# A scan that reads its PSUM tiles with two engines: the masked read first, the plain copy second

## The chip, the cores and the metric

The kernel runs on one core of one Trainium2 chip. The metric is device time in microseconds; the median of three runs is compared. The profile comes from one execution of its own.

## The reference

One layer of a bidirectional diffusion backbone, batch 1, with 128 context tokens and 2048 latent tokens, width 1024, float32. The input is normalised and modulated, and one projection makes all inputs of two groups of channels:

```
h = rmsnorm(x, norm_g) * (1 + scale) + shift
r, k, v, g_a, b_gate, c_gate, u_conv, g_b = split(h @ w_in)
ya = wkv(h, shifted r, k, v, s0) * silu(g_a)      # 8 heads of 64, two directions
yb = b_gate * conv3(c_gate * u_conv) * silu(g_b)  # 512 channels
y  = rmsnorm(x + gate * (concat(ya, yb) @ w_out), final_g)
```

The part that matters here is `wkv`. For each head and each direction it runs a recurrence over the tokens with a state S of 64 x 64, and reads the state out at every token:

```
S = S * w_t - (S kk_t) (kk_t a_t)^T + v_t k_t^T
y_t = S r_t
```

Context tokens start from zero, latent tokens from a given state. The outputs are y for both token sets and the final states of the context.

## The kernel before

Phase 1 (to about 940 us) makes the projections and, per token, the factors of the recurrence, and spills them. Phase 3 (from about 1463 us) is the output projection. Between them lies the scan, `phase2`, which works on chunks of 64 tokens, so that the recurrence inside a chunk becomes matrix products.

The scan has 17 stages. A stage holds, for each of the two directions (`st.g`, two groups `g`), 8 units; a unit is a pair of heads and a chunk. Products of a stage are taken in two halves `n` of 4 units. For each half there are two PSUM tiles per product, one per direction, and they are read out like this:

- F (`partW`, L1017): one masked product on VectorE.
- G (`partW`): for each half `h` of the partitions, ScalarE copies columns 0 to 63 into `fg` (the helper `copy`, L825) and VectorE multiplies columns 64 to 127 with a mask into another slot of `fg` (L1025). A direction's G tile thus has four readers, two on each engine.
- U and W (`partU`): solve inside the chunk. `zr` is a transpose on VectorE (L1031), and `zb` is written by ScalarE (L1048, L823).
- X (`partB`): two negated copies per tile into `fg` on ScalarE (L823).
- E (`partB`): per half two sub-steps, each with one tile per direction. ScalarE copies one set of columns into `E` (L825), VectorE masks the other set (L1086). E has two readers.
- S (`partS`): the recurrence itself. Step `i` multiplies `E` with the state `sv`, and VectorE scales the result into the next unit's `sv` (L1123). The next step's product waits for this.
- `finish` normalises and gates a stage's output y: a square on ScalarE (L1171), a sum on VectorE (L1174), a root on ScalarE (L1175), a reciprocal and a product on VectorE (L1177, L1178), a transpose through TensorE and two more VectorE operations (L1191, L1193).

TensorE's order in the scan is written out by hand: each round r of a stage runs the string

```
ROUND = "f b L L S u b S b S S U S T U S L S B S L B B".split()
```

in which L is a step of F or G of the next stage, b is X or E of this stage's second half, B is X or E of the next stage's first half, u and U are steps of `partU`, S a step of the scan, f and T steps of `finish`. The last rounds use a similar string. So one round has, in TensorE's queue: X, F, G, S, E, S, E, S, S, U, S, (transpose), W, S, F, S, X, S, G, E, E. In what follows psG, psE and so on are the PSUM tiles of these products, and round r is the one whose psU belongs to stage r + 1.

VectorE's and ScalarE's queues are not written by hand. Instructions are recorded in program order and a scheduler places them by its own estimate of when they are ready. When two engines read the same PSUM tile, the one that comes second in the program is made to wait for the one that comes first, also if both only read. In rounds up to the 13th the scan's tiles rotate through five buffers, so the fifth tile after a G tile waits until both engines have read it; then it is three.

From round 12 on ScalarE and VectorE also split the output weights into two parts (`woh` L1330, `wol` L1331) in the same queues, and TensorE begins the output projection (psa).

Of the kernel before, what the change touches and what calls it, by code (L numbers as in the profile page):

```python
# [10 lines left out]
ALU = mybir.AluOpType  # L11
# [25 lines left out]
def place(d, h):  # L37

    x = 1 - h if d == 0 else h
    return slice(x * 64, x * 64 + 64)  # L40
# [708 lines left out]
def phase2(K):  # L749
    nc, tc, A, S = K.nc, K.tc, K.A, K.S  # L750
    V, G, P, T = nc.vector, nc.gpsimd, nc.scalar, nc.tensor
    D = nc.sync.dma_start
    B = Ctx()
# [4 lines left out]
    H = (slice(0, 64), slice(64, 128))  # L758
# [55 lines left out]
    def ps_tile(shape, name):  # L814

        O.n += 1
        if O.pm is not None and (O.n % 5 < 2 or O.p2 is None):
            return O.pm.tile(shape, F32, tag="m", name=name)
        return O.p2.tile(shape, F32, tag="s", name=name)

    def copy(dst, src, negate=False):
        if negate:
            P.activation(dst, src, AF.Copy, scale=-1.0)  # L823
        else:
            P.copy(dst, src)  # L825
# [6 lines left out]
    def mm(*a, **k):  # L832

        r = T.matmul(*a, start=True, stop=True, **k)  # L834
        K.first = r.ins
        if O.line:
            behind(r, O.last)
            O.last = r.ins
# [7 lines left out]
    def tl(shape, tag, b, pool=None, dt=F32):  # L846
        return (pool or O.l0).tile(shape, dt, tag=tag, name=f"{tag}_{K.u()}", bufs=b)
# [8 lines left out]
    def half(g, n):  # L856

        h = n if g.d == 0 else 1 - n
        return slice(h * 4, h * 4 + 4)
# [107 lines left out]
    def load_half(g, us, D):  # L967

        p, c0 = g.units[us.start]
        src = S[f"ops{g.d}"][1:3]  # L970
        for h in range(2):
            dst = B.fg[g.d][H[h], :, g.op, h, us].rearrange("c k u t -> c k (u t)")
            if g.blk is not None:
                D(dst, src[:, p * 128 + h * 64:p * 128 + h * 64 + 64, c0 * 64:(c0 + 4) * 64].rearrange("k c t -> c k t"))
            else:
                for k in range(2):
                    D(dst[:, k].rearrange("c (g t) -> c g t", t=128), src[k, :, 0:128].rearrange("(g h c) t -> h c g t", h=2, c=64)[h][:, p:p + 2])

    def states(s, st):

        D = nc.sync.dma_start if s else P.dma_start
        for g in st.g:
            g.sv = tl([128, 8, 2, 64], "sv", 4)
            load_v(g.sv[64:128], g.units, D)
            first_states(g, D)

    def partW(s, st):

        D = nc.sync.dma_start if s else P.dma_start
        for g in st.g:  # L990
            g.E, g.F = [], []
            g.op = 1 + s % 2
            g.io = slice(0, g.op + 1, g.op)
            g.gs, g.fs = B.fg[g.d][:, 0], B.fg[g.d][:, 1]
        for n in range(2):
            for g in st.g:
                load_half(g, half(g, n), D)
            if n == 0:
                if s:
                    states(s, st)  # L1000
                st.zc = tl([128, 16, 32], "zc", 1, O.r0)
                for h in range(2):
                    D(st.zc[h:128:2], S["zt"][s][h].rearrange("u s b q i -> (s b q) u i"))

            def product(k, x, nm):
                ps = [ps_tile([128, 4, 128], f"ps{nm}{s}_{gi}_{n}") for gi in range(2)]
                for i in range(4):
                    for gi, g in enumerate(st.g):
                        u = half(g, n).start + i
                        for h in range(2):  # L1010
                            mm(ps[gi][place(g.d, h), i, :].rearrange("p (b t) -> p b t", b=2), g.ops[H[h], k, u, :], B.fg[g.d][H[h], x, g.io, h, u])
                return ps

            ps = product(0, 1, "F")
            for gi, g in enumerate(st.g):
                g.F.append(tl([128, 4, 128], "F", 4, O.r0))
                V.tensor_tensor(g.F[n][:], ps[gi][:], B.mF[:, g.d].unsqueeze(1).broadcast_to((128, 4, 128)), ALU.mult)  # L1017
            yield
            ps = product(1, 0, "G")
            for gi, g in enumerate(st.g):  # L1020
                us = half(g, n)
                for h in range(2):
                    r = place(g.d, h)
                    copy(g.gs[H[1 - h], 0, h, us], ps[gi][r, :, 0:64])
                    V.tensor_tensor(g.gs[H[1 - h], g.op, h, us], ps[gi][r, :, 64:128], B.mG[r, g.d].unsqueeze(1).broadcast_to((64, 4, 64)), ALU.mult)  # L1025
            yield

    def partU(s, st):
# [28 lines left out]
    def partB(s, st):  # L1057
        for n in range(2):
            px = [ps_tile([128, 4, 128], f"psX{s}_{gi}_{n}") for gi in range(2)]
            for i in range(4):  # L1060
                for gi, g in enumerate(st.g):
                    u = half(g, n).start + i
                    for h in range(2):
                        r = place(g.d, h)
                        mm(px[gi][H[1 - h], i, :], B.zb[r, gi, u, :], g.F[n][r, i, :])
            for gi, g in enumerate(st.g):
                for h in range(2):
                    copy(g.fs[H[1 - h], g.io, h, half(g, n)], px[gi][H[1 - h]].rearrange("p u (b t) -> p b u t", b=2), True)
            yield
            for h2 in range(2):  # L1070
                for gi, g in enumerate(st.g):
                    if h2 == 0:
                        g.E.append(tl([128, 4, 2, 128], "E", 4))
                    us = half(g, n)
                    k = (h2 if g.d == 0 else 1 - h2) * 2
                    lt, rt = (g.fs, g.gs) if g.d == 0 else (g.gs, g.fs)
                    pe = ps_tile([128, 2, 2, 128], f"psE{s}_{gi}_{n}{h2}")
                    for i in range(2):
                        u = us.start + k + i
                        for hd in range(2):  # L1080
                            for x in range(2):
                                mm(pe[H[x], i, hd, :].rearrange("p (b t) -> p b t", b=2), lt[:, x * g.op, hd, u], rt[:, g.io, hd, u])
                    to = lambda c: g.E[n][:, k:k + 2, :, c].rearrange("p a b c -> p (a b) c")
                    of = lambda c: pe[:].rearrange("p a b c -> p (a b) c")[:, :, c]
                    copy(to(H[0]), of(H[0]))
                    V.tensor_tensor(to(H[1]), of(H[1]), B.mE[:, g.d].unsqueeze(1).broadcast_to((128, 4, 64)), ALU.mult)  # L1086
                yield

    def partS(s, st, nxt):
# [114 lines left out]
    def early():  # L1204
        setup_first()
        center_states()
        partI(2)
        B.back = O.solved
        yield
        sts[0] = partL(0, K.dense)  # L1210
        yield
        partI(3, K.dense)
        yield
        W, uu, bb = partW(0, sts[0]), partU(0, sts[0]), partB(0, sts[0])
        for gen in (W, W, uu, uu, uu):
            next(gen, None)
            yield
        partI(4, B.back)
        for gen in (bb, W, W):
            next(gen, None)  # L1220
            yield
        B.bb = bb

    def main():
# [13 lines left out]
        for s in range(NST):  # L1238
            st = sts.pop(s)
            more = s + 1 < NST  # L1240
            nil = iter(())
            W, uu = (partW(s + 1, sts[s + 1]), partU(s + 1, sts[s + 1])) if more else (nil, nil)
            own, bb = bb, partB(s + 1, sts[s + 1]) if more else nil
            todo = [pend.pop(0) for _ in range(len(pend) if s > NST - 4 else min(1, len(pend)))]
            if s == NST - 3:
# [235 lines left out]
```

## Time and profile before

| | |
|---|---|
| median of 3 runs | 1668.08 us (1666.92 to 1673.68) |
| profiled execution | 1662.38 us |
| its span, first to last instruction | 1660.6 us |
| granted TensorE clock, mean | 0.978 |
| busy: TensorE | 1548.4 us (93%) |
| busy: VectorE | 1077.8 us (65%) |
| busy: ScalarE | 767.6 us (46%) |

In the rows of the profile each line has the start and the length in us, the engine (PE is TensorE, DVE is VectorE, ACT is ScalarE, POOL is GpSimd; PEld is TensorE's loading of weights), the source line, the operation, what it writes and reads, and how many instructions are merged into the row. In square brackets stands how long the engine was idle before it and which engine's work ended the idle time. A row of the waits has who waited, for whom, then us in total, times, and the longest. A float32 matmul shows as two rows in the count. An operation can show as starting a little before the one ahead of it ends.

### The profile page before, as it was taken

The numbers are of one execution on the slowest core, as the hardware profiler recorded it, in microseconds if no ns is written. First come the engines' busy times: TensorE is split into PE (matmuls) and PEld (weight loads), VectorE is DVE, ScalarE is ACT, GpSimd is POOL, SyncE is SP. The second block draws the span as 40 slices with busy tenths as digits, with TensorE's granted clock in tenths as the row PEclk, the third lists the DMA queues.
The fourth block names the chain that finished last, engine by engine and source line by source line (L and its number), as shares of the span: only waits on it lengthen the run. The fifth ranks groups of instructions, "written<-read, shape, count | busy, mean of one in ns | idle before, by whom it ended". The sixth has DMA issues, their size and how long they took to land.

```text
span 1660.6 us, 42386 instructions
## 1 busy us (share of the span) xinstructions
PE 1548.4 (93%) x17160; PEld 1417.8 (85%) x17160; DVE 1077.8 (65%) x2122; ACT 767.6 (46%) x1623; POOL 615.9 (37%) x1134
## 2 busy tenths in 40 slices
PE   6899999999999999999999998988889988789998
PEld 2899998999999999999988997777777877668886
DVE  5876978784638776657788534676767765574343
ACT  4544565553425454435554024666576655432222
POOL 0011221110102111112775588888888840022221
PEclk9899999999999999999999999999999979889999
DMA  9677767665746465555858859566676643264342
GB/s 378 211 258 244 254 236 265 215 227 194 217 145 207 165 207 189 188 201 179 269 177 245 273 180 272 150 184 191 171 211 157 193 135 103 65 198 149 137 146 95
DMA packets 237859, 327.23 MB, mean 197 GB/s; under 512 B 91288, under 2 KB 191896, under 8 KB 223584
## 3 DMA queue, kind: packets, MB, share of 16 engines
q1 hardware_dynamic: 231552, 318.02, 59.6%
q0 software_dynamic: 1360, 4.46, 0.7%
q8 instruction: 135, 2.21, 0.5%
q10 hardware_dynamic: 4752, 2.04, 0.5%
q14 instruction: 60, 0.49, 0.1%
HBM read 207.92 MB, written 116.54 MB: 195 GB/s over the span
## 4 chain that ended last, share of the span: by engine, by line
PE 69%; DVE 14%; ACT 7%; issue 5%; DMA 3%; POOL 0%; SPq 0%; DVEq 0%; ACTq 0%; POOLq 0%
PE psu L1351 4%; PE psu L1350 4%; PE psu L1352 4%; PE psE L834 3%; PE psS L834 3%; ACT fg L823 3%; PE psA L377 2%; PE mmc L166 2%; PE mmc L167 2%; PE mmu L166 2%; PE mmc L168 2%; PE mmu L168 2%; PE mmu L167 2%; PE psX L834 2%; PE mmv L166 2%
## 5 line engine op out<-in xcount | busy, mean ns | idle before, releaser
L939 POOL TENSOR_TENSOR zt<-zt,ztmp 128x30 f32<-128x30 f32 (+7 forms) x450 | 179.5, 399 | 35.1
L834 PE MATMUL psE<-fg 128*64 128x128 f32 x2176 | 137.4, 280 | 20.9 <-DVE fg L1025 17.2
L834 PEld LDWEIGHTS psE<-fg 128*64 128x64 f32 x2176 | 123.1, 141 | 27.3 <-issue 22.0
L834 PE MATMUL psS<-sv,E 128*64 128x64 f32 x2176 | 107.1, 236 | 25.1 <-DVE sv L1123 21.7
L834 PEld LDWEIGHTS psS<-sv,E 128*64 128x64 f32 x2176 | 83.5, 143 | 48.2 <-DVE sv L1123 38.5
L329 POOL TENSOR_TENSOR shk<-rawl 128x384 f32<-128x384 f32 (+1 forms) x24 | 24.9, 1037 | 233.8 <-ACT rawl L325 214.6
L936 POOL TENSOR_TENSOR ztmp<-ab,zt 128x60 f32<-128x60 f32 (+7 forms) x195 | 99.7, 511 | 15.3
L823 ACT ACTIVATE fg<-psX 64x512 f32<-64x512 f32 x136 | 80.5, 592 | 40.5 <-PE psX L834 38.4
L1417 POOL TENSOR_TENSOR z<-z,x 128x512 f32<-128x512 f32 x32 | 41.7, 1303 | 139.4 <-DVE z L1413 114.6
L1123 DVE TENSOR_TENSOR sv<-psS,pc 64x128 f32<-64x128 f32 x254 | 67.8, 279 | 38.8 <-PE psS L834 36.2
L1025 DVE TENSOR_TENSOR fg<-psG,consts 64x256 f32<-64x256 f32 x136 | 56.8, 418 | 47.9 <-ACT fg L825 45.1
L329 POOL TENSOR_TENSOR shv<-rawl 128x384 f32<-128x384 f32 (+1 forms) x24 | 20.4, 852 | 161.9 <-ACT rawl L325 153.7
L825 ACT COPY E<-psE 128x256 f32<-128x256 f32 x136 | 47.7, 374 | 52.6 <-PE psE L834 43.5
L166 PE MATMUL mmg<-h,w 128*128 128x384 f32 (+1 forms) x192 | 63.6, 331 | 3.7 <-ACT q1v L327 3.7
L1017 DVE TENSOR_TENSOR F<-psF,consts 128x512 f32<-128x512 f32 x68 | 44.0, 680 | 34.6 <-PE psF L834 34.6
L166 PE MATMUL mmc<-h,w 128*128 128x384 f32 (+1 forms) x192 | 64.3, 335 | 2.3 <-ACT t L423 1.8
L1086 DVE TENSOR_TENSOR E<-psE,consts 128x256 f32<-128x256 f32 x136 | 54.5, 416 | 18.2 <-ACT E L825 16.7
L825 ACT COPY fg<-psG 64x256 f32<-64x256 f32 x136 | 49.9, 367 | 33.5 <-PE psG L834 16.9
L166 PE MATMUL mmb<-h,w 128*128 128x384 f32 (+1 forms) x192 | 63.1, 329 | 1.5 <-ACT ta L436 1.5
L443 POOL COPY pcs<-pp 128x6 f32<-128x6 f32 (+1 forms) x48 | 21.5, 450 | 115.3 <-ACT pp L432 115.0
L166 PE MATMUL mmgb<-h,w 128*128 128x384 f32 (+1 forms) x192 | 63.7, 332 | 0.3 <-ACT q1r L327 0.3
L166 PE MATMUL mmv<-h,w 128*128 128x384 f32 (+1 forms) x192 | 63.4, 330 | 0.2 <-ACT q1r L327 0.2
(316 smaller groups left out, 5144.9 us busy)
## 6 DMA issues: line engine op xcount, KB each, us to landing
w<-scr_wsp SPq DMA_DIRECT2D x68, 1024.0 KB, 5.5
scr_wsp<-w SPq DMA_DIRECT2D x34, 1024.0 KB, 4.9
scr_ops<-pair SPq DMA_DIRECT2D x80, 384.0 KB, 3.0
wr<-in_win SPq DMA_DIRECT2D x34, 512.0 KB, 5.9
o<-scr_ops SPq DMA_DIRECT2D x32, 512.0 KB, 7.0
fg<-scr_ops SPq DMA_DIRECT2D x120, 128.0 KB, 5.0
x<-in_x SPq DMA_DIRECT2D x17, 512.0 KB, 3.8
wadas<-in_wada SPq DMA_DIRECT2D x8, 1024.0 KB, 13.5
```

What stands on the lines that cost most here:

```text
L166: T.matmul(ps[:, :n], w[:, 0, k], hh[:, 0, k, :n], start=k == 0, stop=False)
L167: T.matmul(ps[:, :n], w[:, 0, k], hh[:, 1, k, :n], start=False, stop=False)
L168: K.dense = T.matmul(ps[:, :n], w[:, 1, k], hh[:, 0, k, :n], start=False, stop=k == 7).ins
L823: P.activation(dst, src, AF.Copy, scale=-1.0)
L825: P.copy(dst, src)
L834: r = T.matmul(*a, start=True, stop=True, **k)
L936: G.tensor_tensor(tv, ab[:, j:j + 2, j + 2:32].unsqueeze(1).broadcast_to((128, kn, 2, n)), zt[:, :kn, j:j + 2].unsqueeze(3).broadcast_to(( ...
L939: O.solved = G.tensor_tensor(zt[:, :kn, j + 2:32], zt[:, :kn, j + 2:32], tv[:, :, r], ALU.subtract).ins
L1123: r = V.tensor_tensor(dst, sp[gi][0:64, q], B.pc[0:64, d, 2 * p:2 * p + 2, c:c + 1].broadcast_to((64, 2, 64)), ALU.mult)
L1350: T.matmul(ps[:], mh[:, n], hi[:, cs], start=start and n == 0, stop=False)
L1351: T.matmul(ps[:], mh[:, n], lo[:, cs], start=False, stop=False)
L1352: T.matmul(ps[:], ml[:, n], hi[:, cs], start=False, stop=stop and n == 3)
```

## The change

In `partW` and in `partB` two statements change places. Each instruction and each access stays as it is.

```diff
                 for h in range(2):
                     r = place(g.d, h)
+                    V.tensor_tensor(g.gs[H[1 - h], g.op, h, us], ps[gi][r, :, 64:128], B.mG[r, g.d].unsqueeze(1).broadcast_to((64, 4, 64)), ALU.mult)
                     copy(g.gs[H[1 - h], 0, h, us], ps[gi][r, :, 0:64])
-                    V.tensor_tensor(g.gs[H[1 - h], g.op, h, us], ps[gi][r, :, 64:128], B.mG[r, g.d].unsqueeze(1).broadcast_to((64, 4, 64)), ALU.mult)
...
+                    V.tensor_tensor(to(H[1]), of(H[1]), B.mE[:, g.d].unsqueeze(1).broadcast_to((128, 4, 64)), ALU.mult)
                     copy(to(H[0]), of(H[0]))
-                    V.tensor_tensor(to(H[1]), of(H[1]), B.mE[:, g.d].unsqueeze(1).broadcast_to((128, 4, 64)), ALU.mult)
```

The mask of G is L1025 before and L1024 after, that of E is L1086 and L1085.

Round 9, VectorE's queue from the first G on (psG_0 and psG_1 are the tiles of the two directions, each twice for the two halves of the partitions; in square brackets the engine whose progress the instruction waits for). Before:

```order
L1025 TENSOR_TENSOR fg_9816<-psG_0_0_15509,consts 64x256 [waits Activation_49]
L1123 TENSOR_TENSOR sv_14984<-psS_0_0_15535,pc 64x128 [waits PE_49]
L1025 TENSOR_TENSOR fg_9817<-psG_1_0_15510,consts 64x256 [waits Activation_49]
L1123 TENSOR_TENSOR sv_14986<-psS_1_0_15541,pc 64x128 [waits PE_49]
L1031 STREAM_TRANSPOSE zr_15547<-zc_15484 128x512 [waits DMAHW6_49,DMAHW0_49]
L1025 TENSOR_TENSOR fg_9816<-psG_0_0_15509,consts 64x256 [waits Activation_49]
L1025 TENSOR_TENSOR fg_9817<-psG_1_0_15510,consts 64x256 [waits Activation_49]
L1086 TENSOR_TENSOR E_15549<-psE_0_10_15550,consts 128x4x64 [waits Activation_49]
L1123 TENSOR_TENSOR sv_14984<-psS_0_0_15535,pc 64x128 [waits PE_49]
L1086 TENSOR_TENSOR E_15561<-psE_1_10_15562,consts 128x4x64 [waits Activation_49]
L1123 TENSOR_TENSOR sv_14986<-psS_1_0_15541,pc 64x128 [waits PE_49]
```

After:

```order
L1024 TENSOR_TENSOR fg_9816<-psG_0_0_15509,consts 64x256 [waits PE_49]
L1024 TENSOR_TENSOR fg_9817<-psG_1_0_15510,consts 64x256 [waits PE_49]
L1123 TENSOR_TENSOR sv_14984<-psS_0_0_15535,pc 64x128 [waits PE_49]
L1123 TENSOR_TENSOR sv_14986<-psS_1_0_15541,pc 64x128 [waits PE_49]
L1024 TENSOR_TENSOR fg_9816<-psG_0_0_15509,consts 64x256 [waits Activation_49]
L1031 STREAM_TRANSPOSE zr_15547<-zc_15484 128x512 [waits DMAHW7_49,DMAHW0_49]
L1024 TENSOR_TENSOR fg_9817<-psG_1_0_15510,consts 64x256 [waits Activation_49]
L1085 TENSOR_TENSOR E_15549<-psE_0_10_15550,consts 128x4x64 [waits PE_49]
L1085 TENSOR_TENSOR E_15561<-psE_1_10_15562,consts 128x4x64 [waits PE_49]
L1123 TENSOR_TENSOR sv_14984<-psS_0_0_15535,pc 64x128 [waits PE_49]
L1123 TENSOR_TENSOR sv_14986<-psS_1_0_15541,pc 64x128 [waits PE_49]
```

The first two masks of G and all masks of E wait for TensorE and no longer for ScalarE; the third and fourth mask of G still wait for a copy. The two masks of a pair now stand together, ahead of the two state updates. The other pair of E behind these rows moves in the same way. ScalarE's queue keeps its order here (four copies of G, four of E), and each of these copies waits for VectorE. TensorE's queue is the same in all rounds up to the 13th.

Round 6, VectorE's queue at the second G, with the normalisation of a finished output (L1174, L1177, L1178). Before:

```order
L1140 TENSOR_TENSOR y_13640<-psS_1_4_14184,y_13640 64x512
L1174 TENSOR_REDUCE yss_14457<-w_14455 128x8
L1025 TENSOR_TENSOR fg_9816<-psG_0_1_14316,consts 64x256
L1025 TENSOR_TENSOR fg_9817<-psG_1_1_14317,consts 64x256
L1177 RECIPROCAL yss_14457<-yss_14457 128x8
L1025 TENSOR_TENSOR fg_9816<-psG_0_1_14316,consts 64x256
L1178 TENSOR_TENSOR y_13647<-y_13647,yss_14457 128x512
L1025 TENSOR_TENSOR fg_9817<-psG_1_1_14317,consts 64x256
```

After:

```order
L1140 TENSOR_TENSOR y_13640<-psS_1_4_14184,y_13640 64x512
L1174 TENSOR_REDUCE yss_14457<-w_14455 128x8
L1177 RECIPROCAL yss_14457<-yss_14457 128x8
L1178 TENSOR_TENSOR y_13647<-y_13647,yss_14457 128x512
L1024 TENSOR_TENSOR fg_9816<-psG_0_1_14316,consts 64x256
L1024 TENSOR_TENSOR fg_9817<-psG_1_1_14317,consts 64x256
L1024 TENSOR_TENSOR fg_9816<-psG_0_1_14316,consts 64x256
L1024 TENSOR_TENSOR fg_9817<-psG_1_1_14317,consts 64x256
```

The reciprocal and the product moved ahead of all four masks, as they stand in rounds 2 and 10 in both kernels. In round 14 it is the other way round: two masks moved ahead of the reciprocal. Where the normalisation falls beside F, it changed places too: the product stands behind both F in rounds 4, 8, 9, 11, 12 and 13 before and in rounds 3, 5, 7, 9 and 11 after.

Round 12, ScalarE's queue at the second G, where the splits of the output weights begin. Before:

```order
L825 COPY fg_9816<-psG_0_1_17227 64x256
L1330 CAST woh_17897<-woraw_17741 128x1024
L825 COPY fg_9817<-psG_1_1_17228 64x256
L825 COPY fg_9816<-psG_0_1_17227 64x256
L825 COPY E_17253<-psE_0_00_17254 128x4x64
L825 COPY fg_9817<-psG_1_1_17228 64x256
L825 COPY E_17265<-psE_1_00_17266 128x4x64
L1330 CAST woh_17953<-woraw_17901 128x1024
L825 COPY E_17253<-psE_0_01_17277 128x4x64
L825 COPY E_17265<-psE_1_01_17288 128x4x64
```

After:

```order
L1330 CAST woh_17897<-woraw_17741 128x1024
L825 COPY fg_9816<-psG_0_1_17227 64x256
L825 COPY fg_9817<-psG_1_1_17228 64x256
L825 COPY E_17253<-psE_0_00_17254 128x4x64
L825 COPY fg_9816<-psG_0_1_17227 64x256
L825 COPY fg_9817<-psG_1_1_17228 64x256
L825 COPY E_17265<-psE_1_00_17266 128x4x64
L825 COPY E_17253<-psE_0_01_17277 128x4x64
L825 COPY E_17265<-psE_1_01_17288 128x4x64
L1330 CAST woh_17953<-woraw_17901 128x1024
```

The first split moved ahead of the copies of G, and the second behind the last copies of E. VectorE's part of the second split (L1331) moved behind its last masks of E in the same way.

## The prediction

> **What bounds the kernel now.** I read the page first, then the waits of the scan (945 to 1465 us), the chain of waits there, and the timeline of one round.
>
> ```profile
> PE 1548.4 (93%) x17160; PEld 1417.8 (85%) x17160; DVE 1077.8 (65%) x2122; ACT 767.6 (46%) x1623; POOL 615.9 (37%) x1134
> PE 69%; DVE 14%; ACT 7%; issue 5%; DMA 3%; POOL 0%; SPq 0%; DVEq 0%; ACTq 0%; POOLq 0%
> ```
>
> TensorE carries 69% of the chain, so only its idle time can be won. VectorE has 14%, and the waits show where:
>
> ```profile
> DVE fg L1025 <- ACT fg L825: 45.1, 30, 3.2
> PEld psS L834 <- DVE sv L1123: 38.2, 80, 2.3
> PE psS L834 <- DVE sv L1123: 21.7, 35, 2.1
> DVE E L1086 <- ACT E L825: 16.7, 23, 3.0
> ```
>
> VectorE stands 61.8 us (45.1 + 16.7) before the two lines that the change moves, and TensorE waits for the state updates (sv, L1123) that stand behind these lines in VectorE's queue. The chain has the same piece in round after round, from zb (L1048) on ScalarE to psU on TensorE:
>
> ```profile
> 1037.43 1.22 ACT zb L1048 x2
> 1044.71 1.15 PE psU L834 x64
> ...
> 1317.45 1.23 ACT zb L1048 x2
> 1324.73 1.13 PE psU L834 x64
> ```
>
> These are the first and the last of ten such pairs, rounds 1 to 12 without 5 and 7, and each takes 7.28 us. A round is some 24.5 us. Round 9 in the timeline, ScalarE, VectorE, TensorE in turn:
>
> ```profile
> 1242.04 1.32 ACT L1048 ACTIVATE zb<-zc,consts 128x512 f32<-128x512 f32 x2
> 1243.39 1.23 ACT L825 COPY fg<-psG 64x256 f32<-64x256 f32 x3
> ...
> 1240.61 1.29 DVE L1017 TENSOR_TENSOR F<-psF,consts 128x512 f32<-128x512 f32 x2 [1.08 <-PE psF L834]
> 1243.79 0.43 DVE L1025 TENSOR_TENSOR fg<-psG,consts 64x256 f32<-64x256 f32 x1 [1.89 <-ACT fg L825]
> 1244.25 0.28 DVE L1123 TENSOR_TENSOR sv<-psS,pc 64x128 f32<-64x128 f32 x1
> 1244.56 0.42 DVE L1025 TENSOR_TENSOR fg<-psG,consts 64x256 f32<-64x256 f32 x1
> 1245.01 0.28 DVE L1123 TENSOR_TENSOR sv<-psS,pc 64x128 f32<-64x128 f32 x1
> 1245.22 0.69 DVE L1031 STREAM_TRANSPOSE zr<-zc 128x512 f32<-128x512 f32 x1
> 1245.84 0.84 DVE L1025 TENSOR_TENSOR fg<-psG,consts 64x256 f32<-64x256 f32 x2
> 1246.71 0.42 DVE L1086 TENSOR_TENSOR E<-psE,consts 128x256 f32<-128x256 f32 x1
> 1247.05 0.27 DVE L1123 TENSOR_TENSOR sv<-psS,pc 64x128 f32<-64x128 f32 x1
> ...
> 1248.64 0.58 DVE L1123 TENSOR_TENSOR sv<-psS,pc 64x128 f32<-64x128 f32 x2
> ...
> 1240.97 1.09 PE L834 MATMUL psG<-fg,o 64*64 64x128 f32 x28 [0.19 <-ACT fg L823]
> 1242.51 1.92 PE L834 MATMUL psE<-fg 128*64 128x128 f32 x32
> 1245.35 0.45 PE L834 MATMUL psS<-sv,E 128*64 128x64 f32 x8 [0.31 <-DVE sv L1123]
> 1245.63 1.92 PE L834 MATMUL psE<-fg 128*64 128x128 f32 x32
> 1247.38 2.04 PE L834 MATMUL psS<-sv,E 128*64 128x64 f32 x32
> 1249.35 1.20 PE L834 MATMUL psU<-zr,a 32*32 32x32 f32 x64
> ```
>
> psG is ready at 1242.06, and VectorE has finished F at 1241.90. Yet it stands idle until 1243.79, because its first mask waits for ScalarE's copy, and ScalarE is still at zb. From then on VectorE works without a gap until 1249.22, and the last state update sets when TensorE reaches psU.
>
> **The change, part by part.** It adds and removes no instruction: 136 copies and 136 masks of each kind stay. The two readers of a PSUM tile are still one after the other; who goes first changes.
>
> 1. The chain from zb to psU, replayed with the durations above. VectorE's first two masks of G now need TensorE alone: 1242.1 to 1242.95, then two sv to 1243.5. All this ran in its idle time. ScalarE's copies start at 1243.39 as before, so the third mask starts at 1243.79 (copy ends 1243.77), transpose from 1244.2, fourth mask to 1245.25, E, E to 1246.1, sv, sv to 1246.6, E to 1246.95. The second psE block, no longer held by the wait of 0.31, ends at about 1246.8, so the last E ends at 1247.3 and the two sv that release the last psS at 1247.85. psU starts at about 1248.3 instead of 1249.35: 1.05 us less. Four operations (two masks, two sv: 0.43 + 0.28 + 0.42 + 0.28 = 1.4 us) left the chain; 0.35 comes back since the sv now stand behind both E of a pair. ScalarE's copies of E then end at 1247.7, before the last psS whose result it copies next (y), so its waits there are hidden. Ten rounds by 1.05 is 10.5. Round 0 keeps two more sv on the chain: 0.7, estimated as 1.05 less what two sv overlap. In rounds 5 and 7 TensorE itself has a hole in this stretch: 0.5 each. Together −12 us; the bounds are 0 (TensorE's next work does not come earlier) and 13 × 1.4 = 18.
>
> 2. The second G and the E after it. There VectorE idles too:
>
> ```profile
> 1235.97 1.33 DVE L1025 TENSOR_TENSOR fg<-psG,consts 64x256 f32<-64x256 f32 x3 [1.67 <-ACT fg L825]
> ```
>
> But the waits of TensorE name no line of this stretch in ordinary rounds; its own psE hide these reads, so the swap costs and wins nothing. Without that cover it would be worth the 1.67 us of a round.
>
> 3. Order of other VectorE work. The scheduler moved the normalisation (reciprocal L1177, product L1178) around F and G. Its price is in the stretches from psU to the next zb, by length (first number) and, third from the end, granted clock; rounds 8, 7, 6, 2 and 10:
>
> ```profile
> 1224.96:1242.14 17.18, 15.78 (x456) 13.93 (x458) 10.85 (x26) 12.98 (x27) 14.95 (x34) 1.00 0.73 208
> 1199.83:1217.68 17.85, 15.56 (x456) 13.85 (x458) 13.26 (x28) 10.86 (x23) 15.38 (x37) 1.00 0.82 234
> 1172.64:1189.52 16.88, 16.00 (x454) 14.04 (x455) 13.29 (x30) 10.56 (x23) 14.57 (x35) 1.00 0.78 205
> 1069.06:1088.85 19.79, 16.36 (x450) 14.75 (x450) 12.05 (x28) 11.94 (x24) 17.22 (x38) 0.91 0.71 197
> 1273.88:1292.99 19.11, 16.82 (x449) 15.24 (x452) 13.44 (x30) 10.65 (x23) 16.47 (x38) 0.91 0.72 182
> ```
>
> Rounds with F first (8: 17.18) against the product first (7: 17.85) differ by 0.67. Rounds 3, 5, 7 gain it, 4, 8, 12, 13 lose it: +0.7. Round 6 had two masks of G ahead of the product (16.88); now the product comes first as in rounds 2 and 10 (19.79, 19.11): +2.6. In rounds 2, 6, 10 TensorE waits for the first G tile to be read out, and the last reader is now the copy, one copy (0.4, a third of the 1.23 of three) later: +1.2. Sum +4.5 us. Its bounds are 0 and 6.
>
> 4. Rounds 12 to 15, where output weights are split on the same two engines:
>
> ```profile
> 1339.49 1.09 PE L834 MATMUL psE<-fg 128*64 128x128 f32 x16 [1.90 <-DVE fg L1025]
> 1344.81 1.76 PE L834 MATMUL psF<-fg,o 64*64 64x128 f32 x26 [2.97 <-DVE E L1086]
> 1375.87 1.09 PE L834 MATMUL psE<-fg 128*64 128x128 f32 x16 [3.10 <-DVE fg L1025]
> 1412.13 4.45 PE L834 MATMUL psE<-fg 128*64 128x128 f32 x48 [3.57 <-DVE fg L1025]
> ```
>
> In round 12 a split of weights (woh on ScalarE, wol on VectorE) stood ahead of the last two reads of E; it now stands behind them, so the wait of 2.97 should go; what is late next is ScalarE's fg from psX, behind the same split, and I leave a third of the wait to it (−2). With the second split the third starts earlier too: −0.5. In round 13 the split starts one copy earlier: −0.5. In round 14 two masks now precede the product: −1. Each of the four waits could also grow by as much as the waits of 1.90 and 2.97 differ (1.1), or go down by twice what I take, so the bounds are +4 and −8. Sum −4 us.
>
> The first stage, beside the last convolutions, I cost at nothing: ScalarE waits longer there, covered by the projections that TensorE still has.
>
> Sum: −12 + 4.5 − 4 = −11.5, and I take −12. The profiled execution took 1662.4 us (span 1660.6), so 1650 against it; the median of the runs shown, 1668.1, stands 5.7 higher, so the forecast is **1656 us**.
>
> The clock is a further cost. After a wait of 1.98 us in round 5 it was half for about 3 us:
>
> ```profile
> 1154.89 0.69 PE L834 MATMUL psS<-sv,E 128*64 128x64 f32 x16 [1.98 <-DVE sv L1123]
> ...
> 1156.00:1159.00 3.00, 3.00 (x44) 2.67 (x38) 1.47 (x4) 2.37 (x7) 2.45 (x8) 0.51 0.76 190
> ```
>
> A dip costs about 1.5 us (half of 3). Waits of that length now stand in rounds 4 and 8 and leave 5 and 7, so I put the net at 0 ± 3. The Trainium skill, "TensorE: Matmul & The Clock Gate", in its tables of limits asks for no gaps over about 3 us between bursts of matmuls. By that rule no wait of 2 us would cost clock and the dips of rounds 4 and 8 would be left out of the range; the trace shows one after 1.98 us (0.51) and so differs.
>
> **The rivals.**
>
> *Nothing measurable (1664).* The gain of part 1 is real, but parts 3 and 4 take it back: round 6, clock dips, a split of weights that lands ahead of a mask: −12 + 6 + 2 = −4. For it: every listed reordering is as large as one round's gain, times two. Against it: only three or four rounds have one, and 13 have the 7.28.
>
> *Slower (1677).* ScalarE, which now stands behind VectorE at each G and E, becomes the engine that is waited for: its fg from psX (L823) and zb come late by one mask per tile pair. Two masks (0.84 us) in 16 rounds, less a third of part 1, would be +13.4 − 4 = +9. It decides where VectorE reaches G later than ScalarE would. The trace speaks against it: VectorE sat idle 1.89 us there for ScalarE, not the other way round, and in the second G it idles too; only the rounds 2, 6, 10 and 12 to 14 have VectorE late.
>
> *The change does less than it says (1667):* psU comes no earlier since TensorE's own stream ends last. From the first psE (1242.51) to psU (1249.35) is 6.84 us. A psE block takes 1.75 us (1245.63 to the next row's start) and a psS group 0.3 (1245.35 to the next), so two blocks and six groups need 5.3: 1.5 us are free, more than the 1.05 claimed.
>
> **How the numbers follow.** Forecast, −8 to −17: chance 0.66. Nothing measurable, by whichever of the two ways: 0.26. Slower: 0.08. A measurement of this kernel can tell about 0.5% (8.3 us) from no change, so the border of faster is 1659.7. The forecast's own range ends just there, so its chance is that of faster: faster 0.66, same 0.26, slower 0.08. The range goes from 1647 (part 1 at 1.4 per round, part 4 at its better end by half) to 1668 (the second case), which leaves out about 0.15.
>
> **What would show it.** Right: the wait of L1025's successor for ScalarE falls from 45 us to a few us, and ScalarE's copies wait for VectorE instead; zb to psU takes 6.2 us in the ten rounds; round 6 stretches to about 19.5 from psU to zb. Wrong, part 1: zb to psU still 7.2 or more, or psU earlier and the next zb not. Wrong, part 4: psE and psF in rounds 12 to 14 wait as long as before or longer.

## The result and the profile after

The changed kernel takes 1658.98 us (median of 7 runs, 1655.87 to 1659.68); the kernel before, run beside it, 1666.92 us (7 runs, 1663.68 to 1673.68). The ratio is 0.9955 with a 95% interval of 0.9934 to 0.9975: 7.5 us less, against the 12 forecast. The gain is there (the interval lies below 1), and at 0.45% it is just short of the 0.5% that the prediction set as the border of "faster".

The profiled executions differ by less than the medians, 1659.7 against 1662.4 us (spans 1657.9 and 1660.6), since the one of before was quicker than all seven runs of that kernel and the one of after the slowest of its seven. So the readings below go by stretches inside the scan, not by the totals. The page after, busy time and chain:

```profile
PE 1545.9 (93%) x17160; PEld 1420.2 (86%) x17160; DVE 1078.8 (65%) x2122; ACT 768.6 (46%) x1623; POOL 615.4 (37%) x1134
PE 70%; DVE 12%; ACT 7%; DMA 5%; issue 5%; POOL 1%; SPq 0%; DVEq 0%; ACTq 0%; POOLq 0%
```

The same work, and a chain in which VectorE has 12% instead of 14 and the transfers 5% instead of 3. The waits of the scan (total, times, longest) say the same:

```profile
ACT fg L825 <- DVE fg L1024: 36.9, 33, 7.3
ACT E L825 <- DVE E L1085: 26.3, 45, 2.5
PEld psS L834 <- DVE sv L1123: 24.1, 41, 1.8
PE psS L834 <- DVE sv L1123: 16.8, 31, 1.6
DVE fg L1024 <- ACT fg L825: 15.3, 16, 3.9
ACT zb L1048 <- DMA zc<-scr_zt: 7.4, 2, 6.6
```

VectorE's wait for ScalarE ahead of the masks of G fell from 45.1 to 15.3 us, TensorE's for the state updates from 21.7 to 16.8 (its weight loads' from 38.2 to 24.1). The prediction's sign was a fall to a few us, so this is met in part. ScalarE now waits for VectorE (36.9 us at G, 26.3 at E), as expected. The last line is new: zb waits for a load.

Round 9 in the timeline, ScalarE, VectorE and TensorE in turn:

```profile
1234.07 1.32 ACT L1048 ACTIVATE zb<-zc,consts 128x512 f32<-128x512 f32 x2
1235.42 1.22 ACT L825 COPY fg<-psG 64x256 f32<-64x256 f32 x3
...
1233.96 0.88 DVE L1024 TENSOR_TENSOR fg<-psG,consts 64x256 f32<-64x256 f32 x2
1234.87 0.48 DVE L1123 TENSOR_TENSOR sv<-psS,pc 64x128 f32<-64x128 f32 x2
1235.82 0.42 DVE L1024 TENSOR_TENSOR fg<-psG,consts 64x256 f32<-64x256 f32 x1 [0.47 <-ACT fg L825]
...
1239.39 0.69 PE L834 MATMUL psS<-sv,E 128*64 128x64 f32 x16 [0.26 <-DVE sv L1123]
1240.01 1.20 PE L834 MATMUL psU<-zr,a 32*32 32x32 f32 x64
```

The first two masks now run while ScalarE is at zb. psU follows zb by 5.94 us; before it was 7.31 (from 1242.04 to 1249.35; the prediction's 7.28 is the same stretch in the rows of the chain).

Then the loss. The chain of the changed kernel from round 9 on:

```profile
1234.17 1.22 ACT zb L1048 x2
1240.08 1.13 PE psU L834 x64
1258.23 1.23 ACT zb L1048 x2
1264.14 1.13 PE psU L834 x64
1290.24 1.33 ACT zb L1048 x2
1296.65 1.13 PE psU L834 x64
```

From psU of round 9 to the next zb it is 18 us, from psU of round 10 to the next zb 26. By the starts of psU the changed kernel was 9.7 us ahead in round 10 (1264.07 against 1273.81) and 3.6 ahead in round 11 (1296.58 against 1300.20).

The reason stands in a queue that the prediction did not look at. GpSimd solves a triangular system per stage (`solve`), some stages ahead of the scan. SyncE loads its input `ab` (L919) into one of two buffers that take turns, and `partI(s + 6)` puts that load at the end of round s. In the same queue stand the loads of the next rounds: `fg` (L974) and `zc` (L1003, the solved system that zb reads). The timeline of SyncE's queue in round 10, changed kernel, and GpSimd's end of a solve:

```profile
1254.04 0.48 SPq L963 DMA_DIRECT2D sv<-scr_vt  x1
1264.56 2.76 SPq L919 DMA_DIRECT2D ab<-scr_at  x4
...
1269.18 13.84 SPq L974 DMA_DIRECT2D fg<-scr_ops  x8
...
1284.92 0.61 SPq L1003 DMA_DIRECT2D zc<-scr_zt  x1
...
1264.22 0.31 POOL L936 TENSOR_TENSOR ztmp<-ab,zt 128x60 f32<-128x60 f32 x1
1265.61 0.61 POOL L940 DMA_DIRECT2D scr_zt<-zt  x1
```

The queue stands from 1254.5 to 1264.56 and moves at once when GpSimd's last read of `ab` (L936) ends. The eight loads of `fg` behind it then take another 13.84 us to issue (11.96 before). A solve takes some 27.6 us (L940 at 1237.91, 1265.61, 1293.14), a round now about 24: the scan catches up with GpSimd's pace until zb has to wait 6.62 us for `zc`:

```profile
1290.24 1.33 ACT L1048 ACTIVATE zb<-zc,consts 128x512 f32<-128x512 f32 x2 [6.62 <-DMA zc<-scr_zt]
```

In the kernel before the queue stood too, but zb needed `zc` only at 1292.90:

```profile
1263.12 2.74 SPq L919 DMA_DIRECT2D ab<-scr_at  x4
...
1282.60 0.61 SPq L1003 DMA_DIRECT2D zc<-scr_zt  x1
```

TensorE's clock adds to it. From psU of round 10 to the next psU the granted clock was 0.84 on average; the kernel before had 0.94 there. Windows of 3 us of the changed kernel in that round (granted clock third from the end):

```profile
1276.00:1279.00 3.00, 1.10 (x20) 0.86 (x17) 2.84 (x8) 1.72 (x5) 2.61 (x6) 1.00 0.74 158
1279.00:1282.00 3.00, 2.19 (x40) 1.62 (x34) 0.79 (x3) 1.93 (x6) 2.61 (x6) 0.56 0.45 126
1282.00:1285.00 3.00, 2.28 (x33) 2.19 (x37) 0.00 (x0) 1.58 (x3) 2.61 (x6) 0.50 0.41 114
```

### The profile page after: what moved, and what is told of

It reads as the page before. It is cut to its first block, busy times and chain, and to the rows that moved or that the text cites. A ratio compares the mean times of both kernels' runs of the same rounds, so it can differ in the third digit from the quotient of the medians.

```text
span 1657.9 us, 42374 instructions
## 1 busy us (share of the span) xinstructions
PE 1545.9 (93%) x17160; PEld 1420.2 (86%) x17160; DVE 1078.8 (65%) x2122; ACT 768.6 (46%) x1623; POOL 615.4 (37%) x1134
## 4 chain that ended last, share of the span: by engine, by line
PE 70%; DVE 12%; ACT 7%; DMA 5%; issue 5%; POOL 1%; SPq 0%; DVEq 0%; ACTq 0%; POOLq 0%
PE psu L1350 4%; PE psu L1351 4%; PE psu L1352 4%; PE psE L834 4%; PE psS L834 3%; PE mmc L166 2%; PE mmc L167 2%; PE mmc L168 2%; PE mmu L166 2%; PE mmu L167 2%; PE mmu L168 2%; PE psA L377 2%; ACT fg L823 2%; PE mmv L166 2%; PE mmv L167 2%
## 5 line engine op out<-in xcount | busy, mean ns | idle before, releaser
L834 PE MATMUL psS<-sv,E 128*64 128x64 f32 x2176 | 100.1, 235 | 19.0 <-DVE sv L1123 16.8
L834 PEld LDWEIGHTS psS<-sv,E 128*64 128x64 f32 x2176 | 82.6, 144 | 35.3 <-DVE sv L1123 24.1
L936 POOL TENSOR_TENSOR ztmp<-ab,zt 128x60 f32<-128x60 f32 (+7 forms) x195 | 102.0, 523 | 15.3
L1123 DVE TENSOR_TENSOR sv<-psS,pc 64x128 f32<-64x128 f32 x254 | 63.8, 277 | 40.8 <-PE psS L834 38.8
L1024 DVE TENSOR_TENSOR fg<-psG,consts 64x256 f32<-64x256 f32 x136 | 57.3, 421 | 26.7 <-ACT fg L825 15.3
L825 ACT COPY fg<-psG 64x256 f32<-64x256 f32 x136 | 49.8, 366 | 42.9 <-DVE fg L1024 36.9
L825 ACT COPY E<-psE 128x256 f32<-128x256 f32 x136 | 48.4, 373 | 37.5 <-DVE E L1085 26.3
L1085 DVE TENSOR_TENSOR E<-psE,consts 128x256 f32<-128x256 f32 x136 | 52.9, 417 | 17.6 <-PE psE L834 16.5
L443 POOL COPY pcs<-pp 128x6 f32<-128x6 f32 (+1 forms) x48 | 21.3, 448 | 114.1 <-ACT pp L432 113.8
```

Of the source, the lines that this page charges most:

```text
L936: G.tensor_tensor(tv, ab[:, j:j + 2, j + 2:32].unsqueeze(1).broadcast_to((128, kn, 2, n)), zt[:, :kn, j:j + 2].unsqueeze(3).broadcast_to(( ...
L1123: r = V.tensor_tensor(dst, sp[gi][0:64, q], B.pc[0:64, d, 2 * p:2 * p + 2, c:c + 1].broadcast_to((64, 2, 64)), ALU.mult)
```

## The experiments

Theory A: the gain is that of the stretch from zb to psU, and it is given back because SyncE's queue waits for GpSimd's solves. Theory B: it is given back by the order that the scheduler gave to the normalisation and to the weight splits, which differ between the kernels; GpSimd has no part in it.

All ten, each beside new runs of the kernel before (medians 1668.3 to 1669.5), times in us. The third column of numbers is the stretch from zb to psU in an ordinary round, the last one the four rounds from psU of round 7 to psU of round 11; four solves take 110.

| kernel | median | ratio to before (95%) | zb to psU | four rounds |
|---|---|---|---|---|
| before | 1666.9 | 1 | 7.31 | 100.4 |
| changed | 1659.0 | 0.9955 (0.9934 to 0.9975) | 5.94 | 106.3 |
| G swapped alone | 1661.9 | 0.9938 (0.9917 to 0.9959) | 6.18 | 104.9 |
| E swapped alone | 1666.9 | 0.9986 (0.9963 to 1.0008) | 7.34 | 100.5 |
| changed, later load | 1647.9 | 0.9874 (0.9840 to 0.9908) | 5.94 | 95.9 |
| before, later load | 1668.4 | 1.0005 (0.9983 to 1.0027) | 7.31 | 102.8 |
| changed, `ab` by GpSimd | 1692.2 | 1.0147 (1.0113 to 1.0182) | 5.95 | 104.6 |
| G alone, later load | 1652.5 | 0.9910 (0.9879 to 0.9940) | 6.18 | 98.6 |
| changed, later load, masks first | 1645.2 | 0.9858 (0.9827 to 0.9888) | 5.95 | 94.7 |
| changed, short solve | 1648.0 | 0.9881 (0.9846 to 0.9916) | 5.94 | 104.4 |
| changed, masks first | 1662.5 | 0.9954 (0.9932 to 0.9976) | 5.94 | 113.8 |
| before, long solve | 1680.8 | 1.0074 (1.0049 to 1.0099) | 7.30 | 115.4 |

**G alone.** The two lines of G from the changed kernel, those of E from the kernel before.

> The kernel before with VectorE's masked read first for G alone; E as it was. Two theories. A: the gain is made in the stretch from ScalarE's write of zb to psU, 1.37 us a round (7.31 to 5.94), where the masked halves of the second G tiles used to wait for ScalarE's copies; it is given back in round 10 (7.1 us) because SyncE's queue stands behind the load of ab, which waits for GpSimd's solves of 27.6 us a stage. B: the loss has nothing to do with GpSimd; it comes from the order that the scheduler gave the normalisation and the last rounds' weight splits, which differ between the kernels. Here the instruction order of TensorE, GpSimd and SyncE outside the very last rounds is that of the kernel before. A expects the stretch at 6.0 to 6.5 in most rounds, GpSimd's limit to bite in a late round all the same, and the time at 1658 to 1662. B expects no late loss, since the order of the normalisation is the old one, and 1651 to 1655.

1661.88 us. The stretch is 6.18 us, and round 10 is long all the same (28.9 us to the next psU, after 27.3 for round 9), with the normalisation in the old order. The time is the one that A named and not that of B, and SyncE's queue is held here too (`zc` issues at 1287.77, 15.8 us after psU of round 10). But zb waits for no load in this execution. The two long rounds hold waits of TensorE that name no releaser, 2.79 us at 1250.90 and 2.48 at 1279.55, and a lower clock after them; how the late queue costs time here is not shown.

**E alone.** The two lines of E from the changed kernel, those of G from the kernel before.

> The changed kernel with G's two reads put back (ScalarE's copy first); only E is swapped. A expects the stretch from zb to psU at 7.0 to 7.3 in most rounds, no long wait for the loads of fg and zc in round 10, and a time within 2 us of the kernel before, 1665 to 1669. B expects the disturbances of the new order without the gain, so a time above the kernel before: 1669 to 1673. If the stretch falls to about 6 here, the gain is E's and not G's.

1666.85 us, a stretch of 7.34, no long round 10 (25.9). E's swap by itself is worth nothing measurable; the gain is G's, as A expected.

**The later load**, in the changed kernel and in the kernel before:

```diff
-            if 1 <= s and s + 6 < NST:
-                partI(s + 6)
+            x = s + 6 if s < 6 else s + 5
+            if 1 <= s and s != 6 and x < NST:
+                partI(x)
```

> The changed kernel with the load of ab and the solve of a stage put one round later in the program from round 7 on, so that SyncE's queue reaches the load when GpSimd has already freed the buffer. The same work on every engine. A expects GpSimd's waits to leave SyncE's queue: the loads of fg and zc issue 9 to 12 us earlier in round 10, psU of round 11 comes 24 us after that of round 10 instead of 32.5, and the kernel is 6 to 9 us faster than the changed one: 1650 to 1653. B expects no more than 2 us, since neither the normalisation nor the weight splits are touched: 1657 to 1659.

1647.89 us, 2 to 5 us faster than A expected. SyncE's queue in round 9 and 10 of this kernel:

```profile
1250.35 2.74 SPq L919 DMA_DIRECT2D ab<-scr_at  x4
...
1268.48 0.70 SPq L1003 DMA_DIRECT2D zc<-scr_zt  x1
```

`zc` issues 3.8 us after psU of round 10 (1264.73), in the changed kernel 20.9 after (1264.07). The next psU comes 25.4 us after, not 32.5. GpSimd's solves keep their pace (27.6 to 28.1 us each), so what changed is where the load stands in the queue. Over the four rounds it is 10.3 us faster than the changed kernel, and over rounds 11 to 14 another 7.6; the scan of this execution began 3 us later and its early rounds took 0.8 longer. The two ratios differ by some 13 us (0.0081 of 1667, with about 0.004, or 7 us, either way). The part in rounds 11 to 14 can't be put down to the queue: over the kernels of the table without the run that loads `ab` by GpSimd, these four rounds took 121 to 130 us with no clear tie to it.

> The kernel before with the same later place of ab's load and solve from round 7 on. In the kernel before the rounds of 24.4 us leave the blocked queue some slack (zc's load issued 8.7 us after psU in round 10), so A expects nothing here: within 2 us of the kernel before, 1665 to 1668, which makes the gain of the later load one that only the faster order can use. B expects the same of this one. If it is 4 us or more faster than before, the queue was already limiting the kernel before and the later load is a gain of its own.

1668.39 us: nothing. The kernel before loses no time to its queue; the faster order does. This pair is the plainest evidence for A: the same edit is worth nothing measurable in the one order and some 13 us in the other.

**`ab` loaded by GpSimd.**

```diff
-                behind(D(dst, src), after)
+                behind((G.dma_start if s >= 7 else D)(dst, src), after)
```

> The changed kernel with the load of ab from stage 7 on issued by GpSimd instead of SyncE; its place in the program, the solves and every other instruction stay. It asks whether it is SyncE's queue behind that load that costs round 10 its time, or whether the run with the later load gained by something else that moved (the solves start later there too). Queue theory: SyncE is never held by the solves, zc of round 10 issues within 6 us of psU, the step from psU of round 10 to that of round 11 falls from 32.5 to 24 or 25, and the kernel is 8 to 12 us faster than the changed one, 1647 to 1651. If it is the place of the solves in time instead (their traffic or their memory accesses beside the round's work), nothing changes: 1657 to 1661.

1692.23 us, a miss. GpSimd now issues a load right ahead of the solve that needs it and stands until it lands:

```profile
1213.95 1.96 POOL L919 DMA_DIRECT2D ab<-scr_at  x4
1222.02 0.20 POOL L928 COPY dgp<-ab 128x16 f32<-128x16 f32 x1 [6.11 <-DMA ab<-scr_at]
```

A solve thus takes 32 to 37 us instead of 27.6 (L940 at 1176.04, 1213.07, 1248.87, 1281.03), and its results come too late themselves: that of 1281.03 is what `zc` of round 10 loads at 1283.57. Rounds 6 to 9, before that, took 23.1 to 26.2 us. So it took the block from SyncE and made GpSimd the bound. It says nothing between the theories. The Trainium skill, "DMA: Bandwidth & Descriptors", section "Issuing engines are not separate DMA queues", says that issuing from several engines saves only the sequencer's time to issue, usually little. Here where a load stands cost far more than its issue (1.96 us): the two places of `ab` that these runs tried changed the time by some −13 and +32 us.

**G alone with the later load.** The edits of G alone and of the later load together.

> G's swap alone (E as before) with the later load of ab. It prices E's swap once SyncE's queue is out of the way. The normalisation of a finished tile stands behind the second G masks in round 6 here and ahead of them in the changed kernel, which cost that round 1.9 us (the step from psU of round 6 to that of round 7 was 23.7 with G alone, 25.6 with both). Against that the stretch from zb to psU is 6.18 with G alone and 5.94 with both, 0.24 a round for eleven rounds, 2.6 in all. Queue theory: the late loss is gone here too, 8 to 11 us below G alone, 1650 to 1654, and within 3 us of both swaps with the later load (1648). Should the order of the normalisation decide most, this one is 3 us or more faster than both swaps: 1645 or less.

1652.51 us, 9 below G alone by the medians and 5 by the ratios (0.9910 and 0.9938, with overlapping intervals), and the long round 10 is gone (25.1). It is 5 us more than both swaps with the later load, where at most 3 were expected, though these two intervals overlap as well. It is not faster than both swaps, so the order of the normalisation was not the larger effect.

**Later load, masks first.** Beside the later load, on the changed order:

```diff
-                    V.tensor_tensor(g.gs[H[1 - h], g.op, h, us], ps[gi][r, :, 64:128], B.mG[r, g.d].unsqueeze(1).broadcast_to((64, 4, 64)), ALU.mult)
+                    O.mask = V.tensor_tensor(g.gs[H[1 - h], g.op, h, us], ps[gi][r, :, 64:128], B.mG[r, g.d].unsqueeze(1).broadcast_to((64, 4, 64)), ALU.mult).ins
...
-        V.tensor_reduce(ss[:], heads(w[:]), mybir.AxisListType.X, ALU.add)
+        behind(V.tensor_reduce(ss[:], heads(w[:]), mybir.AxisListType.X, ALU.add), O.mask)
```

> Both swaps, the later load of ab, and the sum that begins the normalisation held behind the last G mask on VectorE, so that the masks come first in every round. With the later load alone rounds 2, 6 and 10, where the normalisation stands first, took 28.9, 25.5 and 25.4 us against 23.2 to 23.8 in the others. The order theory expects rounds 6 and 10 at 23.3 to 23.8 and round 2 shorter by 2 to 4, so 5 to 7 us less than the later load alone: 1641 to 1643. If it is the round's other work that makes these three long (the waits for the normalisation's square on ScalarE, a dip of the clock), no more than 1 us: 1647 to 1649.

1645.20 us. Rounds 2, 6 and 10 went from 28.9, 25.5 and 25.4 to 24.9, 23.0 and 23.1 us, 8.8 together, as the order theory had it. The median is lower by only 2.7, below what the two intervals tell apart, where the order theory named 5 to 7. It is the fastest kernel of the study.

**Short solve**, on the changed kernel:

```diff
-        for m in range(15):
+        for m in range(15 if s < 7 else 9):
```

> The changed kernel with the triangular solve cut to the first 9 of its 15 steps from stage 7 on, so that GpSimd needs about 18 us a stage instead of 27.6 and the buffer of ab is free earlier; order and places are those of the changed kernel, and the computation is left incomplete. Queue theory: as fast as with the later load, 1647 to 1651, with the step from psU of round 10 to that of round 11 at 24 to 25. The other theory, that the late loss is made by the scheduler's order and not by GpSimd's pace: 1657 to 1661 with the step still above 30.

1647.97 us, as A had it: by the median a quicker GpSimd does as much as the later load. Round 10 took 25.7 us, a little over the 24 to 25 that A named. The four rounds are not as short as there. Of the 8.5 us between them 3.8 are a hole ahead of psU of round 10, which the chain gives to no releaser:

```profile
1259.93 3.77 issue
```

Another such hole is 1.45 us (at 1212.02), and the granted clock over the four rounds is 0.95 instead of 1.00. In this execution most of the lead over the changed kernel, 8 of 10.6 us, arose in rounds 11 to 14, so here the median speaks for A and the rounds alone do not.

**Masks first, load unchanged.** The edit that puts the masks first, without the later load.

> The changed kernel with the normalisation held behind the last G mask on VectorE, and the load of ab where the change left it. Without SyncE's queue in the way this order took 8.8 us out of rounds 2, 6 and 10 (28.9, 25.5 and 25.4 us to 24.9, 23.0 and 23.1). Queue theory: GpSimd's pace sets when round 10 gets its loads, so whatever rounds 2 and 6 save is waited for in round 10: psU of round 11 comes within 2 us of 1296.6 plus the shift of the scan's start, and the time stays within 2 us of the changed kernel, 1657 to 1661. If savings in single rounds add up whatever the queue does, it is 4 to 8 us faster than the changed kernel: 1651 to 1655.

1662.45 us beside 1668.28 before: the ratio of the changed kernel to the third digit (0.9954 and 0.9955). The early rounds are short, and rounds 7 to 10 then take 26.3, 27.8, 30.2 and 29.5 us, on average a little over GpSimd's 27.6. The shift went further than expected, psU of round 11 at 1303.77 instead of about 1299. Here it is VectorE that waits for SyncE's queue, for `w` (L1161), which stands a few loads behind the held one of `ab` (1242.39 after 1238.20, 1270.65 after 1265.88). From 1190 to 1304 us:

```profile
DVE yo L1193 <- DMA w<-scr_q: 13.2, 4, 6.0
```

TensorE's stream has three holes of 2.1 to 3.5 us there besides. Savings ahead of the queue are waited for behind it.

**Long solve in the kernel before.**

```diff
-        G.tensor_tensor(tv, ab[:, :, 0:32:2], dg[:].unsqueeze(1).broadcast_to((128, 32, 16)), ALU.mult)
+        [G.tensor_tensor(tv, ab[:, :, 0:32:2], dg[:].unsqueeze(1).broadcast_to((128, 32, 16)), ALU.mult) for _ in range(1 if s < 7 else 3)]
```

> The kernel before with 2.6 us more work on GpSimd in every solve from stage 7 on (its 1.30 us multiplication by the diagonal is done three times, with the same result); the order of instructions on the other engines and in SyncE's queue is that of the kernel before. By round 10 the buffer of ab is free 7 x 2.6 = 18 us later. In the kernel before the second zc load was issued at 1283.96 for a zb at 1292.90, and takes 3.6 us to land, so some 5 us of slack. Queue theory: the slack is used up and the rest waited for, 10 to 16 us slower than before, 1678 to 1684, with ScalarE's zb of round 11 waiting for zc. If GpSimd is off the path of the scan, as its share of the chain in the kernel before says, the time is that of the kernel before within 2 us: 1665 to 1670.

1680.80 us. GpSimd's rows:

```profile
1254.65 0.61 POOL L940 DMA_DIRECT2D scr_zt<-zt  x1
1256.17 4.05 POOL L931 TENSOR_TENSOR ztmp<-ab,dgp 128x512 f32<-128x512 f32 x3
...
1285.15 0.61 POOL L940 DMA_DIRECT2D scr_zt<-zt  x1
```

A solve takes 30.5 us here, and rounds 7 to 10 took 27.5, 29.2, 29.0 and 29.6 instead of 24.5 to 26.4. GpSimd, with no share of the chain in the kernel before, limits the time once its solve is 2.9 us longer. The expected wait of zb for `zc` does not show. Rounds 8, 9 and 10 each hold a hole in TensorE's stream without a releaser (2.06, 1.59 and 1.91 us), and the granted clock over the four rounds is 0.90 instead of 0.98; the path from GpSimd's pace to these is not shown.

## Why the prediction was right in its range and too large in its size

**Part 1 (zb to psU, 12 us): right, and somewhat small.** Over the ten rounds named the stretch shortened by 11.6 us where 10.5 was forecast: 1.37 in an ordinary round instead of 1.05, nothing in round 1. G's swap alone gives 1.13 of it. 5.94 is close to the 5.8 that the third rival's bound allowed (7.31 less 1.5 free). Part of the rest is TensorE's second psE block: it starts 2.68 us after zb instead of 3.59, 0.9 earlier, where the replay had it end some 0.75 earlier (1246.8 instead of 1247.55). In round 7 a hole of 2.17 us in TensorE's stream, which the kernel before had there, was absent; that is not the change's.

**Part 2 (second G and E, nothing): not contradicted.** The stretch from psU to the next zb, which holds them, is 17.15 us in undisturbed rounds of both kernels (8 and 9 before, 5 after). E's swap alone gives a ratio of 0.9986 with 1 in its interval.

**Part 3 (order of the normalisation, +4.5): right in the round that carried it, too small in round 2, far off in round 10.** From psU to the next zb round 6 went from 16.95 to 19.02 (forecast +2.6, about 19.5), round 2 from 19.76 to 21.86 (forecast a third of +1.2). Round 3 gained 0.5, as forecast, and round 8 lost 1.7 instead of 0.67; round 7 lost 1.1 where 0.67 was to be won. In rounds 7 and 8 TensorE's stream has holes of 1.62 and 1.96 us that name no releaser, so these two rounds don't price the order. Taking the normalisation out of the masks' way gave 8.8 us back in rounds 2, 6 and 10, though rounds 2 and 10 had that order before too, so that not all of it is the change's. Round 10, forecast at +0.4, lost 7.1.

**Part 4 (weight splits, −4): wrong in its mechanism.** From psU of round 12 to that of round 15 the kernel took 102.7 us before and 105.5 after, one execution each; the other kernels (without the run that loads `ab` by GpSimd) took 97.9 to 104.5, so the sign of the sum is not settled. TensorE's long waits in this stretch, after:

```profile
1330.12 0.77 PE L834 MATMUL psS<-sv,E 128*64 128x64 f32 x16 [1.57 <-DVE sv L1123]
1349.25 1.97 PE L834 MATMUL psE<-fg 128*64 128x128 f32 x16 [3.67 <-ACT fg L825]
1372.32 1.09 PE L834 MATMUL psE<-fg 128*64 128x128 f32 x16 [2.32 <-ACT fg L825]
1410.01 5.39 PE L834 MATMUL psE<-fg 128*64 128x128 f32 x48 [4.80 <-ACT E L825]
```

psF's wait of 2.97 is gone, as forecast. But the waits that named VectorE's masks (1.90, 3.10, 3.57) now name ScalarE's copies (3.67, 2.32, 4.80). Where both engines are late, the second reader still ends last, and swapping the two only changes its name. That is the mechanism of the slower rival, in rounds that the prediction had named as those with VectorE late. The stretch was quicker with the later load (98.8 us) and with the short solve (97.9), but also with the long solve in the kernel before (98.9); why, was not tried.

**What was missed.** The step that failed is the sum: that each round's gain adds up. It took as fixed when the loads arrive, and looked neither at SyncE's queue nor at GpSimd's pace, which stood in the trace of before at 27.4 to 28.4 us a solve against rounds of 24.5, with 37% busy on the page as an average. Rounds 7 to 10 took 106.3 us after against 100.4 before, although each has at least 1.37 less in part 1; the pair with the later load puts the price of the queue at some 13 us in all. With the later load the change is worth about 21 us (ratio 0.9874), not 12; without it some 13 of these are lost. So the forecast landed in its range by two errors of opposite sign, which is luck. Of the 9 us that it had too little the larger part 1 is about 1; the rest can't be placed, since single rounds vary by holes of 2 to 4 us and rounds 12 to 14 by 7.

That the place of the load and GpSimd's pace decide this is shown by the times: later load, short solve and long solve each move them clear of their intervals, and the later load does nothing in the slower order. How a late load costs TensorE its time is seen only in part: through zb's wait for `zc` in round 10 of the changed kernel, and through VectorE's wait for `w` with the masks first. The holes in TensorE's stream are larger in the four rounds of the kernels whose queue is held (4.9 us changed, 7.6 G alone) than with the later load (0.7), but the short solve has 5.2 us of them too. The lower end of the range, 1647, comes to about 1648 from the terms named for it.

**The rivals.** Of the three, "nothing measurable" came nearest: the gain is real and partly taken back, and at 0.45% the time lies just on its side of the border of 0.5%. It named round 6, the clock and a weight split as the takers; round 6 took 2.1 us and the rounds of the splits 2.9 in this pair of executions, but the largest taker, round 10, was not among them. "Slower" and "does less than it says" are excluded by the interval and by the 5.94 us.

**The clock (0 ± 3).** In round 10 it fell to 0.56 and 0.50 for 6 us, after a wait of 1.90 us of TensorE for ScalarE's fg (psE at 1278.24). In rounds 4 and 8, where the forecast expected dips, the granted clock was 1.00 from psU to psU. Of rounds 1 to 11 it was lower in 2, 6 and 10 (0.88, 0.93 and 0.84); the kernel before had 0.94 in rounds 2, 5, 6 and 10. The dip of round 5 is gone, as forecast. The Trainium skill, "TensorE: Matmul & The Clock Gate", section "HAM oscillation — how this bites in real kernels", puts the limit at idle gaps of more than about 3.4 us. No such single gap is listed in that round, so here too the trace differs.

## What to carry to other kernels

When two engines read the same tile one after the other, let the one go first that idles there and that the bound engine waits for; read that from the waits, tile by tile, and expect nothing where both are late. Before adding up a gain per round, look for every queue and every engine that runs ahead at a pace of its own, and compare its period with the shortened round: an engine that is 37% busy over the whole kernel can be the bound of one stage. A load whose buffer comes free at another engine's pace belongs at the place in an in-order queue where the buffer is already free; moving it by one round was worth more here than the change itself.

## What the runs showed of the hardware that was not expected

- Neither the length of one wait nor the share of work in the 3 us before it tells alone whether TensorE's clock falls. Windows of 3 us up to the end of such a wait and behind it, first of the changed kernel (a wait of 1.90 us, psE at 1278.24), then with the later load (1.86 us, psE at 1279.65):

```profile
1275.24:1278.24 3.00, 1.10 (x20) 0.86 (x15) 2.84 (x6) 1.09 (x3) 2.61 (x6) 1.00 0.87 186
1278.24:1281.24 3.00, 2.95 (x48) 2.37 (x48) 1.52 (x5) 1.81 (x6) 2.61 (x6) 0.69 0.46 117
...
1276.65:1279.65 3.00, 1.14 (x20) 0.90 (x17) 2.62 (x6) 1.29 (x4) 2.53 (x6) 1.00 0.65 183
1279.65:1282.65 3.00, 3.00 (x84) 2.81 (x84) 1.52 (x5) 2.60 (x7) 2.61 (x6) 1.00 0.85 224
```

  TensorE was busy for 1.10 and 1.14 of 3 us; the clock fell behind the first wait and stayed at 1.00 behind the second. It also stayed at 1.00 in round 8 of the changed kernel, after a longer wait (1.96 us, ended at 1222.91) and a window (1221 to 1224) with 1.09 of 3 us busy. What decides is open.

- TensorE has holes of up to 4 us in the middle of a run of like products that name no releaser, here in round 8 of the changed kernel:

```profile
1222.91 0.68 PE L834 MATMUL psS<-sv,E 128*64 128x64 f32 x14 [1.96 <-issue]
```

  They come back near the same places in several kernels: in psW of round 9 (changed, G alone, long solve), in psF of round 10 (G alone, masks first, long solve). They move a profiled execution by as much as the terms of the sum. In the twelve traces, all 64 such holes of 0.5 us or more between 1010 and 1440 us end 1.25 to 1.88 us after a transfer of 16 KB has landed on the DMA queue of the kind "instruction" (q8 on the page); the one above ends at 1222.91, the transfer at 1221.50. These transfers land every 5 to 6 us on average, so chance would not do it: TensorE seems to wait for its own instructions. No run tried this.
